# A hybrid decoder step: transposes one projection tile behind, block products ahead of the last ones, six projection banks, and reordered seams in the down projection

## The chip, the cores and the metric

The kernel runs on one core of a Trainium2 chip. The metric is the device time of one execution in microseconds; the median of three runs of the kernel before is 1769.6 us (1768.57 to 1771.12). Lower is better.

## What is computed

The reference is one inference step of a decoder layer for a prompt of 1024 rows and a sample group of 64 rows (8 sequences of 8), model width 1024, in fp32. What matters here is its second part:

```python
x = x + merged @ w_out                                   # output projection
f, conv_state = conv_ffn(rmsnorm(x, norm2_g), ...)       # see below
x = x + f
y = rmsnorm(x, final_norm_g)

def conv_ffn(h, prefix, w_gate, w_up, conv_w, conv_b, w_down):
    g = h @ w_gate                                       # 1024 x 2816
    u = h @ w_up
    gc = conv_b + sum_j conv_w[j] * shifted(g, j)        # causal, width 3
    return (gelu(gc) * u) @ w_down, last two rows of g
```

## The kernel before

**Products.** Each fp32 operand is split into a high part (a cast on ScalarE, L113) and a low part (a subtraction on VectorE, L114). A product runs three passes on TensorE: high by high, high by low, low by high. A weight or activation tile that was split lies in a slot of the tag hl (five slots); what was loaded for it lies in a slot of the tag raw (four slots). Results are summed in PSUM. Until the gate/up loop ends there are two tiles of two banks (tag big), two of one bank (nat), and one each of tp and av, which the transposes use.

**Output projection and second norm (from L950 on).** For each half `nb` of the 1024 output columns the sample (`mm_s`) and the eight prompt tiles (`mm_n`, 24 products each) are projected, each into a nat bank. `add_sq` adds the bank to the residual x (VectorE, L931) and sums its squares on ScalarE (L932), which writes its unused result into the bank. In the second half each tile is then stored to `x1_d` for the end of the kernel, `norm2` normalises it in place (`rstd_of`, seven steps on [128,1] and a square root, then L938), and `put` transposes it, 128 columns at a time, into the stacks B11, B21, B22 and T1 to T4. B are quadrants of the normalised activations; T are sums and differences of them (L989 to L992 on VectorE and GpSimd), since the products use a seven-product scheme on 2 x 2 blocks. T1 and T2 take the slots that the first four tiles' inputs leave, T3 and T4 those of the others. The tiles come in the order 0, 2, 1, 3, 4, 6, 5, 7.

**Gate/up loop.** For 22 rounds `m`, `prep(m)` splits the seven weight pieces a11, s1, s2, a12, s3, s4, a22 (the sums and differences on GpSimd) and `products(m)` runs the block products (`prod`, L1132, 12 TensorE products each) in the order a11 by B11, s1 by T1, s2 by T2, a12 by B21, s3 by T3, s4 by B22, a22 by T4, with ScalarE copies and VectorE adds between them. The products of s1 go to the bank that the code calls c.

**Down projection (`run_steps`).** Seven passes P1, P2, P5, P6, P7, P3, P4, each of 11 steps (k), each step four row tiles of three products (L1298) into four banks of a new pool of seven; P2, P6, P7 and P3 add two products per step for the sample (L1338, bank sb). `prep_down` loads and splits a step four steps ahead. The first four steps of P1 run from raw slots (`k < 4`); the others from the tiles XB and ST, which lie where the loop's pools were. `sum1` and `sum2` form sums and differences for later passes. `evac` takes a pass's banks out: the first at the end of the pass, the others one per step in the next. The banks of P7 are the ones of P6; P3 and P4 take new ones. After P3 the first four row tiles and the sample are normalised (`norm`: ScalarE scales, GpSimd multiplies by the gain and stores). In P4 the last four steps are held back and run row tile by row tile, each followed by its norm on VectorE and its stores.

**What sets the order.** The order on each engine and on the queues of SP and GpSimd is fixed when the kernel is built. A planner takes the source order as priority, and puts an instruction earlier if by its own estimate of times it is ready while those ahead of it are not. On the chip each engine keeps that order.

Of the kernel before, what the change touches and what calls it, by code (L numbers as in the profile page):

```python
# [16 lines left out]
P = 128  # L17
# [15 lines left out]
def hybrid_step(ctx, tc, x_prompt, x_sample, mem_prompt, cache_k, cache_v, page_table, state_pool,  # L33
# [888 lines left out]
    with tc.tile_pool(name="p5", bufs=1, reuse_waits="tile") as p5:  # L922
# [11 lines left out]
        def norm2(xt, n, t):  # L934
# [3 lines left out]
            nc.vector.scalar_tensor_tensor(xt, xt, r, g2b[:n], op0=ALU.mult, op1=ALU.mult)  # L938
# [3 lines left out]
        def put(Bt, xh, a, wide=False):  # L942
# [5 lines left out]
            split(Bt[:, 0, :, a * P:(a + 1) * P], Bt[:, 1, :, a * P:(a + 1) * P], v)  # L948

# [3 lines left out]
        for nb in range(2):  # L953
# [6 lines left out]
            else:  # L960
                nc.sync.dma_start(g2b, bc(norm2_g[0], P))
                raws[0], raws[1] = raw_ffn(0), raw_ffn(1)
            pt = nat()
            mm_s(pt, wf, ms)
            add_sq(x1s, (pt[0:TS], pt[TS:P]), pt[0:TS], TS, NT, nb)
            if nb == 1:
                nc.gpsimd.dma_start(x1s_d, x1s)
                norm2(x1s, TS, NT)
                xs = ap_.tile([P, KT, P], F32R, tag="hs", bufs=1, name="xs")
                to_stack(x1s, xs, KT)  # L970
                nc.gpsimd.tensor_tensor(x1s[:, 0:512], x1s[:, 512:D], x1s[:, 0:512], op=ALU.subtract)
            for i, t in enumerate((0, 2, 1, 3, 4, 6, 5, 7) if nb else range(NT)):
                pt = nat()
                mm_n(pt, wf, macts, t)
                add_sq(x1[t], (pt,), pt, P, t, nb)
                if nb == 0:
                    continue
                nc.gpsimd.dma_start(x1_d[t], x1[t])
                norm2(x1[t], P, t)
                if i == 3:  # L980
                    T1, T2 = [ap_.tile([P, 2, 4, 512], F32R, tag="act", bufs=4, name=f"T{q}") for q in (1, 2)]
                a = t // 2
                if t % 2 == 0:
                    put(B11, x1[t][:, 0:512], a)
                    put(B21, x1[t][:, 512:D], a)
                    continue
                xa, xb = x1[t - 1], x1[t]
                put(B22, xb[:, 512:D], a)
                nc.vector.tensor_tensor(xa[:, 0:512], xb[:, 0:512], xa[:, 0:512], op=ALU.subtract)  # L989
                nc.gpsimd.tensor_tensor(xb[:, 0:512], xb[:, 512:D], xb[:, 0:512], op=ALU.subtract)  # L990
                nc.vector.tensor_tensor(xb[:, 512:D], xb[:, 512:D], xa[:, 0:512], op=ALU.subtract)
                nc.gpsimd.tensor_tensor(xa[:, 512:D], xa[:, 512:D], xb[:, 512:D], op=ALU.subtract)  # L992
                todo.append((xa, xb, a))
                if T1 is not None:
                    for (xa, xb, a) in todo:
                        put(T1, xa[:, 0:512], a)
                        put(T2, xb[:, 512:D], a)
                        late.append((xa, xb, a))
                    todo = []
# [9 lines left out]
    with tc.tile_pool(name="fa", bufs=1, reuse_waits="tile") as fa:  # L1009
# [70 lines left out]
        def prep(m):  # L1080
# [14 lines left out]
            tA = pair("wA")  # L1095
            w["a11"] = piece(tA, 0, a11)
# [10 lines left out]
            w["a12"] = piece(tA, 1, a12)  # L1107
# [21 lines left out]
        def prod(out, wt, Bt, start):  # L1129
            for k in range(4):  # L1130
                for (pw, ph) in PASSES:
                    nc.tensor.matmul(out, wt[:, pw, k], Bt[:, ph, k], start=(start and k == 0 and (pw, ph) == (0, 0)),  # L1132
                                     stop=(k == 3 and (pw, ph) == (1, 0)), skip_group_check=True)

        def products(m, nxt):
            w = wts.pop(m)
            ab = big()
# [12 lines left out]
            prod(a, w["a11"], B11, True)  # L1150
# [8 lines left out]
            prod(b, w["a12"], B21, True)  # L1159
# [70 lines left out]
        def sum1(k):  # L1230
            ld(ST[k][:, 0], fA(1, 1, k))
            if k < 4:
                ld(ST[k][:, 1], wB(0, 0, k))
# [3 lines left out]
        def sum2(k):  # L1237
            if k < 4:
# [9 lines left out]
        def sq(x, junk, i, c):  # L1248
            n = x.shape[0]
            nc.scalar.activation(junk, x, AF.Square, accum_out=ssf[:n, i, c:c + 1])  # L1250

        def norm(x, i, dst, late):
            n = x.shape[0]
            ss = sm.tile([P, 1], F32, tag="ss", name=f"ss{uid()}")[:n]
            tt(ss, ssf[:n, i, 0:1], ssf[:n, i, 1:2], ALU.add)
            r = rstd_of(ss, n, 1.0 / D, 1)
            if late:
                for c in (LO, HI):
                    nc.vector.scalar_tensor_tensor(x[:, c], x[:, c], r, gfb[:n, c], op0=ALU.mult, op1=ALU.mult)
                    nc.sync.dma_start(dst[:, c], x[:, c])  # L1260
            else:
                nc.scalar.activation(x, x, AF.Identity, scale=r)
                nc.gpsimd.tensor_tensor(x, x, gfb[:n], op=ALU.mult)
                nc.gpsimd.dma_start(dst, x)

        def smp2(c, op):
            for h in range(2):
                tt(ys[:, c], ys[:, c], sb[0][h * TS:(h + 1) * TS], op)

        def evac(p, t, b):  # L1270
            y0, y1 = Y[t], Y[t + 4]
            if p == "P1":
                nc.scalar.copy(U[t], b)
            elif p == "P2":
                tt(y0[:, LO], y0[:, LO], b, ALU.add)
                sq(y0[:, LO], b, t, 0)
# [205 lines left out]
```

## Time and profile before

| | |
|---|---|
| median of 3 runs | 1769.6 us |
| profiled execution | 1768.74 us |
| its span, first to last instruction | 1767.0 us |
| mean granted TensorE clock | 0.986 |
| TensorE busy | 1698.4 us, 96% |
| VectorE busy | 952.8 us, 54% |
| ScalarE busy | 723.2 us, 41% |
| GpSimd busy | 412.1 us, 23% |
| chain that ended last, TensorE's share | 84% |

Times in the profile are microseconds from the first instruction. PE is TensorE, DVE is VectorE, ACT is ScalarE, POOL is GpSimd, SP the engine that issues most loads; L12 is line 12 of the kernel. An idle time is put down to what ended it. Products are pipelined, so a run of them is read by its length and count, not by the duration of one.

### The profile page before, as it was taken

The numbers are of one execution on the slowest core, as the hardware profiler recorded it, in microseconds if no ns is written. First come the engines' busy times: TensorE is split into PE (matmuls) and PEld (weight loads), VectorE is DVE, ScalarE is ACT, GpSimd is POOL, SyncE is SP. The second block draws the span as 40 slices with busy tenths as digits, with TensorE's granted clock in tenths as the row PEclk, the third lists the DMA queues.
The fourth block names the chain that finished last, engine by engine and source line by source line (L and its number), as shares of the span: only waits on it lengthen the run. The fifth ranks groups of instructions, "written<-read, shape, count | busy, mean of one in ns | idle before, by whom it ended". The sixth has DMA issues, their size and how long they took to land.

```text
span 1767.0 us, 22904 instructions
## 1 busy us (share of the span) xinstructions
PE 1698.4 (96%) x8157; PEld 1327.8 (75%) x8157; DVE 952.8 (54%) x1648; ACT 723.2 (41%) x1397; POOL 412.1 (23%) x438
## 2 busy tenths in 40 slices
PE   7999999999999999999989899999999999899996
PEld 5887876765666787777768778888888888688875
DVE  6412134330220766676734776666666666578778
ACT  5422234331330766665522354444444444344343
POOL 1113020300200324202200244444444442100003
PEclk9999999999999999999999999999999999999998
DMA  7432251357665424154542132222222222891513
GB/s 272 152 131 82 79 171 59 110 180 237 201 223 193 136 86 142 34 167 155 182 167 66 72 63 72 73 73 73 73 73 72 73 73 84 299 337 49 177 68 137
DMA packets 142359, 228.18 MB, mean 129 GB/s; under 512 B 26703, under 2 KB 64109, under 8 KB 142245
## 3 DMA queue, kind: packets, MB, share of 16 engines
q1 hardware_dynamic: 126453, 178.25, 31.3%
q0 software_dynamic: 15792, 48.48, 8.1%
q8 instruction: 64, 1.05, 0.2%
q14 instruction: 50, 0.41, 0.1%
HBM read 176.19 MB, written 50.54 MB: 128 GB/s over the span
## 4 chain that ended last, share of the span: by engine, by line
PE 84%; DVE 6%; DMA 3%; issue 3%; ACT 2%; SPq 1%; POOL 1%; DVEq 0%; POOLq 0%; ACTq 0%
PE nat L182 18%; PE big L1132 17%; PE P L1298 10%; PE nat L191 8%; PE nat L1132 7%; PE big L182 4%; PE tp L110 4%; PE av L1047 3%; PE big L781 2%; PE av L811 2%; PE nat L199 2%; PE av L110 1%; PE av L571 1%; PE sb L1338 1%; PE big L675 1%
## 5 line engine op out<-in xcount | busy, mean ns | idle before, releaser
L182 PE MATMUL nat<-act,hl 128*128 128x512 f32 x1344 | 359.3, 405 | 0.0
L182 PEld LDWEIGHTS nat<-act,hl 128*128 128x128 f32 x1344 | 242.7, 189 | 62.1 <-issue 15.1
L1298 PE MATMUL P<-hd 128*128 128x512 f32 x924 | 223.7, 397 | 12.9 <-ACT hd L113 6.1
L1298 PEld LDWEIGHTS P<-hd 128*128 128x128 f32 x924 | 176.7, 192 | 52.5 <-ACT hd L113 6.7
L191 PE MATMUL nat<-hl,act 128*128 128x512 f32 x768 | 187.6, 402 | 6.8 <-ACT nat L932 5.1
L191 PEld LDWEIGHTS nat<-hl,act 128*128 128x128 f32 x768 | 146.9, 193 | 39.0 <-ACT nat L932 5.5
L1132 PE MATMUL big<-B,wA 128*128 128x512 f32 x528 | 131.2, 396 | 0.0
L114 DVE TENSOR_TENSOR hl<-raw,hl 128x1024 fp32r<-128x1024 f32 x52 | 66.4, 1288 | 117.1 <-ACT hl L113 115.8
L1132 PEld LDWEIGHTS big<-B,wA 128*128 128x128 f32 x528 | 95.9, 188 | 24.4 <-ACT gu L1157 6.3
L114 DVE TENSOR_TENSOR wB<-stm,wB 128x512 fp32r<-128x512 f32 x44 | 50.7, 1154 | 102.1 <-ACT wB L113 102.1
L474 POOL DMA_DIRECT2D gl<-ev x48 | 26.2, 547 | 280.8 <-ACT ev L473 256.5
L473 ACT COPY ev<-nat 128x512 f32<-128x512 f32 x48 | 28.1, 586 | 116.1 <-PE nat L182 115.6
L1115 POOL TENSOR_TENSOR stm<-rf,stm 128x512 f32<-128x512 f32 x22 | 28.7, 1304 | 188.3 <-DVE wB L114 188.2
L1132 PE MATMUL nat<-B,wC 128*128 128x512 f32 x264 | 70.5, 389 | 0.0
L113 ACT CAST hl<-raw 128x1024 fp32r<-128x1024 f32 x60 | 62.5, 1051 | 16.8 <-PE nat L182 7.9
L1132 PE MATMUL big<-T,wC 128*128 128x512 f32 x264 | 66.4, 400 | 0.0
L114 DVE TENSOR_TENSOR hd<-rd,hd 128x1024 fp32r<-128x1024 f32 x37 | 49.3, 1334 | 30.2 <-ACT hd L113 25.9
L1132 PE MATMUL nat<-T,wB 128*128 128x512 f32 x264 | 64.9, 394 | 0.0
L1132 PE MATMUL big<-T,wD 128*128 128x512 f32 x264 | 64.0, 391 | 0.0
L113 ACT CAST hd<-rd 128x1024 fp32r<-128x1024 f32 x37 | 38.9, 1051 | 60.1 <-PE sb L1338 31.9
L1132 PE MATMUL big<-T,wB 128*128 128x512 f32 x264 | 63.4, 389 | 0.0
L1148 DVE TENSOR_TENSOR gu<-gu,big 128x512 f32<-128x512 f32 x44 | 30.3, 688 | 57.2 <-PE big L1132 57.2
(450 smaller groups left out, 3168.8 us busy)
## 6 DMA issues: line engine op xcount, KB each, us to landing
raw<-in_w_in SPq DMA_DIRECT2D x40, 512.0 KB
kr<-in_cache_k SPq DMA_DIRECT2D x64, 256.0 KB
vr<-in_cache_v SPq DMA_DIRECT2D x64, 256.0 KB
rd<-f_d SPq DMA_DIRECT2D x59, 256.0 KB
gl<-ev POOLq DMA_DIRECT2D x48, 256.0 KB, 2.7
rd<-in_w_ffn_down SPq DMA_DIRECT2D x48, 256.0 KB
rf<-in_w_ffn_gate SPq DMA_DIRECT2D x22, 512.0 KB
rf<-in_w_ffn_up SPq DMA_DIRECT2D x22, 512.0 KB
```

Source lines behind the costliest of these rows:

```text
L110: nc.tensor.transpose(out, in_, ident[:n, :n])
L113: nc.scalar.copy(hi, src)
L114: (lo_eng or nc.vector).tensor_tensor(lo, src, hi.bitcast(F32), op=ALU.subtract)
L182: nc.tensor.matmul(out, wf(k, pw)[:, n0:n0 + P], acts[c][ph][:, k, :], start=(k == ks[0] and (pw, ph) == (0, 0)), stop=(k == ks[-1] and (p ...
L191: nc.tensor.matmul(out, acts[c][ph][:, k, o:o + P], wf(k, pw), start=(k == ks[0] and (pw, ph) == (0, 0)), stop=(k == ks[-1] and (pw, ph) = ...
L199: nc.tensor.matmul(out, stack[:, k, :], wf(k, pw), start=(k == ks[0] and pw == 0), stop=(k == ks[-1] and pw == 1))
L781: nc.tensor.matmul(S[:, k0:k0 + n], Qd[:, m, part, qs], Kst[:, m, k0:k0 + n], start=(part == 0), stop=(part == 1))
L811: nc.tensor.matmul(av[:, :P], aT[:, k * P:(k + 1) * P], vn[:, k0 + k], start=(k0 + k == 0), stop=(k0 + k == i))
L1047: nc.tensor.matmul(pt[:, i * 256:(i + 1) * 256].rearrange("p (h x) -> p h x", h=2), xs[:, k] if k < 4 else st2[:, k - 4], w[n1][:, :, k] i ...
L1132: nc.tensor.matmul(out, wt[:, pw, k], Bt[:, ph, k], start=(start and k == 0 and (pw, ph) == (0, 0)), stop=(k == 3 and (pw, ph) == (1, 0)), ...
L1148: nc.vector.tensor_tensor(hv(g, i), hv(g, i), q(x), op=ALU.add)
L1298: nc.tensor.matmul(banks[t], h[:, ph, 0, t * P:(t + 1) * P], h[:, pw, 1], start=(k == 0 and p not in ("P2", "P7") and (pw, ph) == (0, 0)), ...
```

## The change

In the first half of the output projection, sample and tiles take six banks in turn (two nat, four halves of the two big tiles), and each half of x1 is stored by itself as it is done. In the second half the sum goes to a staging tile `stg` (two of the four raw slots), which the norm reads and which is stored; the loads for the up matrix's first round, so far issued ahead of this half, come with `prep(0)`. The transposes of a tile are written in the source after the next tile's projection, add and norm. Ahead of the last tile's transposes stand the split of a11 and a12 and their two block products of the first round.

In the down projection five steps of P1 (not four) run from raw slots; one step (not four) is written ahead of the sample's leftovers; `evac` hands out single operations, which `more` takes, four at the first step of a pass and one or two at the others; P7's squares no longer go through each bank; the four first norms of P3 are one chain of [128,4] steps, and the scaling is one VectorE instruction with no GpSimd multiply; P4's right halves are multiplied by the gain beforehand, and its norms split the scaling between ScalarE and VectorE.

```diff
-        def add_sq(xt, pts, junk, n, t, nb):
+        def add_sq(xt, pts, junk, n, t, nb, out=None):
             xh = xt[:, nb * 512:(nb + 1) * 512]
+            out = xh if out is None else out
             for q in pts:
-                nc.vector.tensor_tensor(xh, xh, q, op=ALU.add)
-            nc.scalar.activation(junk, xh, AF.Square, accum_out=ssn[:n, t, nb:nb + 1])
+                nc.vector.tensor_tensor(out, xh, q, op=ALU.add)
+            nc.scalar.activation(junk, out, AF.Square, accum_out=ssn[:n, t, nb:nb + 1])
...
+            for (c, src) in ((slice(0, 512), xt[:, 0:512]), (slice(512, D), hi)):
+                nc.vector.scalar_tensor_tensor(xt[:, c], src, r, g2b[:n, c], op0=ALU.mult, op1=ALU.mult)
+        def obank(nb):
+            obc[0] += 1
+            if nb or obc[0] % 6 in (1, 2):
+                return nat()
+            if not obs:
+                pt = big()
+                obs.extend((pt[:, 0], pt[:, 1]))
+            return obs.pop(0)
...
-                raws[0], raws[1] = raw_ffn(0), raw_ffn(1)
-            pt = nat()
+                raws[0] = raw_ffn(0)
+                stg = [wp.tile([P, 2, 512], F32, tag="raw", bufs=4, name=f"stg{i}") for i in range(2)]
+            pt = obank(nb)
...
             for i, t in enumerate((0, 2, 1, 3, 4, 6, 5, 7) if nb else range(NT)):
-                pt = nat()
+                pt = obank(nb)
                 mm_n(pt, wf, macts, t)
-                add_sq(x1[t], (pt,), pt, P, t, nb)
                 if nb == 0:
+                    add_sq(x1[t], (pt,), pt, P, t, nb)
+                    nc.gpsimd.dma_start(x1_d[t][:, 0:512], x1[t][:, 0:512])
                     continue
-                nc.gpsimd.dma_start(x1_d[t], x1[t])
-                norm2(x1[t], P, t)
+                hi = stg[i % 4 // 2][:, i % 2]
+                add_sq(x1[t], (pt,), pt, P, t, nb, hi)
+                nc.gpsimd.dma_start(x1_d[t][:, 512:D], hi)
+                norm2(x1[t], P, t, hi)
+                if i == 6:
+                    tA0 = wp.tile([P, 2, 2, 4, P], F32R, tag="hl", bufs=5, name="wA0")
+                    for q in range(2):
+                        split(tA0[:, q, 0], tA0[:, q, 1], raws[0][q][:, :, 0:P])
+                behind.pop()()
...
+                if i == 7:
+                    ab0 = big()
+                    prod(ab0[:, 0], tA0[:, 0], B11, True)
+                    prod(ab0[:, 1], tA0[:, 1], B21, True)
+                def puts(t=t, a=t // 2):
...
+                behind.append(puts)
+        behind.pop()()
...
-                if k < 4:
+                if k < 5:
                     src = rawt(fA(0, 0, k), wB(0, 0, k))
...
+        def norm(xs_, i, dsts):
+            n, w = xs_[0].shape[0], len(xs_)
+            ss = sm.tile([P, w], F32, tag=f"rs_s{w}", bufs=1, name=f"ss{uid()}")[:n]
+            tt(ss, ssf[:n, 0, i:i + w], ssf[:n, 1, i:i + w], ALU.add)
+            r = rstd_of(ss, n, 1.0 / D, w)
+            for j, (x, dst) in enumerate(zip(xs_, dsts)):
+                def go(x=x, dst=dst, j=j):
+                    nc.vector.scalar_tensor_tensor(x, x, r[:, j:j + 1], gfb[:n], op0=ALU.mult, op1=ALU.mult)
+                    nc.gpsimd.dma_start(dst, x)
+                yield go
+        def last(t, b):
+            y, i = Y[t + 4], t + 4
+            tt(y[:, LO], y[:, LO], b, ALU.add)
+            sq(y[:, LO], b, i, 0)
...
+            nc.scalar.activation(y[:, HI], y[:, HI], AF.Identity, scale=r)
+            nc.sync.dma_start(dst[:, HI], y[:, HI])
+            nc.vector.scalar_tensor_tensor(y[:, LO], y[:, LO], r, gfb[:, LO], op0=ALU.mult, op1=ALU.mult)
+            nc.sync.dma_start(dst[:, LO], y[:, LO])
...
             elif p == "P7":
-                tt(U[t], U[t], b, ALU.add)
-                tt(y1[:, HI], y1[:, HI], U[t], ALU.subtract)
-                sq(y1[:, HI], b, t + 4, 1)
-                tt(y1[:, LO], y1[:, LO], U[t], ALU.add)
+                yield lambda: tt(U[0], U[0], bk[0], A)
+                for h in range(2):
+                    yield lambda h=h: smp1(LO, S, h, sbk)
+                    yield lambda h=h: smp1(HI, A, h, sbk)
+                for t in range(1, 4):
+                    yield lambda t=t: tt(U[t], U[t], bk[t], A)
+                for t in range(4):
+                    yield lambda t=t: tt(Y[t + 4][:, HI], Y[t + 4][:, HI], U[t], S)
+                    yield lambda t=t: (sq(Y[t + 4][:, HI], bk[3], t + 4, 1), tt(Y[t + 4][:, LO], Y[t + 4][:, LO], U[t], A))
+                sq(ys[:, LO], bk[3][0:TS], NT, 0)
             elif p == "P3":
...
+                yield from norm([Y[t] for t in range(4)], 0, [y_prompt[t * P:(t + 1) * P] for t in range(4)])
+                for t in range(4):
+                    yield lambda t=t: tt(Y[t + 4][:, HI], Y[t + 4][:, HI], gfb[:, HI], ALU.mult)
+                nc.vector.tensor_scalar(ssf[:, 1, 4:8], ssf[:, 1, 4:8], 1.0 / D, EPS, op0=ALU.mult, op1=A)
+                yield from norm([ys], NT, [y_sample])
...
-                    if pend:
-                        evac(*pend.pop(0))
+                    more(4 if k == 0 else 1 if p != "P3" and p != "P4" or k > 6 else 2)
...
-        run_steps(0, 4)
+        prep_down(4)
+        run_steps(0, 1)
```

## Rows read from the trace of the kernel before

**Rows 1.** Waits, TensorE: engine, line, releaser; total us, times, longest.

```profile
PE P L1298 <- ACT hd L113: 6.1, 2, 5.6
PE nat L191 <- ACT nat L932: 5.1, 1, 5.1
PE P L1298 <- DVE hd L114: 4.5, 2, 4.3
PE av L110 <- DVE x L938: 2.9, 1, 2.9
PE P L1298 <- ACT P L1250: 2.3, 1, 2.3
```

**Rows 2.** Stretches: length, busy us (instructions) of each engine, granted clock, DMA.

```profile
908.00:912.00 4.00, 3.81 (x9) 3.04 (x10) 0.00 (x0) 0.75 (x4) 0.00 (x0) 0.50 1.03 411
...
949.18:1032.88 83.70, 74.52 (x373) 59.28 (x372) 61.97 (x130) 31.85 (x71) 25.02 (x24) 0.96 0.27 73
...
1030.00:1490.00 460.00, 459.60 (x2164) 372.06 (x2162) 292.56 (x375) 197.71 (x363) 190.27 (x168) 1.00 0.25 75
...
1520.00:1590.00 70.00, 65.03 (x279) 53.51 (x280) 52.76 (x55) 32.55 (x47) 1.07 (x2) 0.95 0.98 348
```

**Rows 3.** TensorE in order of time, projection: start, us, operation, count, idle before.

```profile
908.19 41.16 PE L191 MATMUL nat<-hl,act 128*128 128x512 f32 x168 [5.11 <-ACT nat L932]
...
1008.34 0.71 PE L1132 MATMUL big<-B,wA 128*128 128x512 f32 x2
...
1027.07 1.06 PE L1132 MATMUL nat<-T,wB 128*128 128x512 f32 x2
...
1032.88 2.88 PE L1132 MATMUL big<-T,wB 128*128 128x512 f32 x12
```

**Rows 4.** VectorE in order of time, around the last projection tile.

```profile
1010.01 0.68 DVE L931 TENSOR_TENSOR x<-x,nat 128x512 f32<-128x512 f32 x1
...
1015.02 1.28 DVE L938 SCALAR_TENSOR_TENSOR x<-x,rsy,g2b 128x1024 f32<-128x1024 f32 x1
```

**Rows 5.** TensorE in order of time, down projection.

```profile
1507.06 11.34 PE L1298 MATMUL P<-hd 128*128 128x512 f32 x48
...
1524.97 23.81 PE L1298 MATMUL P<-hd 128*128 128x512 f32 x96 [5.57 <-ACT hd L113]
...
1580.80 32.80 PE L1298 MATMUL P<-hd 128*128 128x512 f32 x144
...
1685.34 6.86 PE L1298 MATMUL P<-hd 128*128 128x512 f32 x22 [2.32 <-ACT P L1250]
...
1719.69 20.11 PE L1298 MATMUL P<-hd 128*128 128x512 f32 x88
...
1746.04 11.64 PE L1298 MATMUL P<-hd 128*128 128x512 f32 x41 [4.34 <-DVE hd L114]
```

**Rows 6.** ScalarE in order of time, casts of XB in the first down pass.

```profile
1523.79 0.61 ACT L113 CAST hd<-XB 128x512 fp32r<-128x512 f32 x1
...
1531.13 0.62 ACT L113 CAST hd<-XB 128x512 fp32r<-128x512 f32 x1 [1.44 <-DMA XB<-f_d]
```

**Rows 7.** VectorE in order of time, from the seam of P7 to the end.

```profile
1682.65 1.28 DVE L1197 TENSOR_TENSOR uy<-uy,P 128x512 f32<-128x512 f32 x2
...
1738.69 1.22 DVE L114 TENSOR_TENSOR hd<-rd,hd 128x1024 fp32r<-128x1024 f32 x1
...
1742.62 4.50 DVE L114 TENSOR_TENSOR hd<-rd,hd 128x1024 fp32r<-128x1024 f32 x2
...
1760.73 0.15 DVE L1197 TENSOR_TENSOR ss<-ssf 128x1 f32<-128x1 f32 x1
```

**Rows 8.** Groups by line, 1712 to 1768: busy us, mean ns; idle before.

```profile
L1263 POOL TENSOR_TENSOR yy<-yy,uy 128x1024 f32<-128x1024 f32 x4 | 11.5, 2894 | 205.5 <-ACT rst L121 205.1 <-ACT yy L1262 0.4
L1259 DVE SCALAR_TENSOR_TENSOR yy<-yy,rsy,uy 128x512 f32<-128x512 f32 x8 | 5.6, 747 | 0.1
```

**Rows 9.** Groups by line, GpSimd, 949 to 1033, the same columns.

```profile
L990 POOL TENSOR_TENSOR x<-x 128x512 f32<-128x512 f32 x4 | 5.1, 1287 | 15.3 <-DVE x L989 15.3
```

More of the change, by code (lines that the diff above doesn't have):

```diff
@@ L948, in put, with prod @@
             split(Bt[:, 0, :, a * P:(a + 1) * P], Bt[:, 1, :, a * P:(a + 1) * P], v)
+        def prod(out, wt, Bt, start):
+            for k in range(4):
+                for (pw, ph) in PASSES:
+                    nc.tensor.matmul(out, wt[:, pw, k], Bt[:, ph, k], start=(start and k == 0 and (pw, ph) == (0, 0)),
+                                     stop=(k == 3 and (pw, ph) == (1, 0)), skip_group_check=True)
         raws = {}
@@ L1094, in prep @@
             w = wts[m] = {}
-            tA = pair("wA")
-            w["a11"] = piece(tA, 0, a11)
+            tA = pair("wA") if m else tA0
+            w["a11"] = piece(tA, 0, a11) if m else tA[:, 0]
             yield
@@ L1106, in prep @@
             yield
-            w["a12"] = piece(tA, 1, a12)
+            w["a12"] = piece(tA, 1, a12) if m else tA[:, 1]
             yield
@@ L1127, in prep @@
             late_s.extend([smp_])
[L1129 to L1133, printed above, removed]
         def products(m, nxt):
             w = wts.pop(m)
-            ab = big()
+            ab = big() if m else ab0
             a, b, c = ab[:, 0], ab[:, 1], nat()
@@ L1158, in products @@
             next(nxt, None)
-            prod(b, w["a12"], B21, True)
+            if m:
+                prod(b, w["a12"], B21, True)
             acc(g0, 0, b)
@@ L1249, in sq @@
             n = x.shape[0]
[L1250 to L1264, printed above, removed]
@@ L1300, in mm4, with more @@
                                  stop=(k == KH - 1 and (pw, ph) == (1, 0)), skip_group_check=True)
+        def more(n):
+            while n and pend:
+                f = next(pend[0], None)
+                if f is None:
+                    pend.pop(0)
+                    continue
+                f()
+                n -= 1
         def run_steps(s0, s1):
-            for g in range(4, s0 + 4 if s0 else 0):
-                prep_down(g)
             for s in range(s0, s1):
@@ L1341, in run_steps @@
                     continue
-                now = 4 if p in ("P1", "P6") else 1
-                for t in range(4):
-                    if t < now:
-                        evac(p, t, banks[t])
-                    else:
-                        pend.append((p, t, banks[t]))
-                if p == "P6":
-                    smp2(LO, ALU.add)
-                if p == "P7":
-                    smp2(LO, ALU.subtract)
-                    smp2(HI, ALU.add)
-                    sq(ys[:, LO], sb[0][0:TS], NT, 0)
-                if p == "P3":
-                    smp2(HI, ALU.add)
-                    sq(ys[:, HI], sb[0][0:TS], NT, 1)
-                    norm(ys, NT, y_sample, False)
+                pend.append(evac(p, list(banks), sb[0]))
+                more(1)
             if s1 == len(steps):
@@ L1361, in run_steps @@
                         mm4("P4", k, t, h)
-                    evac("P4", t, banks[t])
+                    if t == 0:
+                        more(99)
+                    last(t, banks[t])
         S1AT = {4 + (13 * k) // 10: k for k in range(KH)}
```

111 lines of the change are left out of this document (65 added, 46 removed).

## The prediction

> **What bounds the kernel now.** TensorE does. First I read the stretches [rows 2]: in the gate/up loop it is busy 459.60 of 460 us at full clock, with VectorE at 292.56 and GpSimd at 190.27. What comes off ahead of the loop moves the end one for one, and nothing inside it can be had. So I looked where TensorE waits [rows 1]: one wait of 5.1 us on ScalarE at L932 (the output projection), 2.9 us on VectorE at L938 (the second norm), 5.6 us on ScalarE's cast at L113 and 2.3 us at L1250, 4.3 us on VectorE's split at L114 (the down projection). Then its order in time [rows 3, 5] shows a second loss behind each long wait. The pace at full clock is 144 products in 32.80 us [rows 5], 0.227 us each; after the 5.1 us wait 168 products take 41.16 us [rows 3], 3.0 more than 38.1, and the granted clock there is 0.50, the 1.2 GHz level, against 2.4 [rows 2]. After the 2.3 us wait 22 products take 6.86 us instead of 5.0 (1.9 lost), after the one at L113 96 take 23.81 instead of 21.8 (2.0 lost), after the last 41 take 11.64 instead of 9.3 (2.3 lost) [rows 5]. I count wait and slow stretch together.
>
> **The change part by part.** The sum is against the profiled execution, 1768.74 us (span 1767.0).
>
> *Six banks in the first half of the projection.* The second prompt tile has to wait for the sample's bank, which waits for x_sample to land: 5.11 us, then 3.0 at the low clock [rows 3]. Now the sample and tile 0 sit in the two nat banks, tiles 1 to 4 in four halves of two big banks; the first reuse is tile 5, some 5 x 5.45 = 27 us after tile 0 starts, long past the 5.1 us. The big tiles are free: the gate stage's last products are over before. Eight stores of 256 KB are added on GpSimd's queue, idle here, and the second half's become half as large. Gain 8.1; if the clock fell all the same 5.1.
>
> *Transposes one tile behind, two block products ahead of the last ones.* The stretch from the second half's first product to 1032.88, where TensorE becomes continuous, is 83.70 us: TensorE busy 74.52, so 9.2 waiting, VectorE 61.97 [rows 2]. The last projection product ends at about 1008.2. VectorE adds that tile only at 1010.01 (splits of earlier transposes stand ahead of it) and has it normalised at 1015.02 + 1.28 = 1016.3, 8 us later [rows 4]; product c starts at 1027.07, 19 us after the projection [rows 3]. After the change add and norm come ahead of the previous tile's transposes: 0.69 + a square + seven small steps + 1.3, about 5 us. Under them TensorE has 24 block products (5.4 us; 12 of them are there now, as the row at 1008.34 shows) and the transposes of the tile before. What VectorE then has to do until c is the last pair's two differences, its three splits, T3 and T4's eight, the sample's and one weight's: the whole between projection and c sums, with the norm, to some 19 splits, adds and differences at 0.61 (0.69 less the overlap of 0.08 with the next), plus 2.0 for norm and small steps: 13.6, say 14 us with gaps, against 19. So: 5.0 from the chain, 2.7 for the a12 product (12 x 0.227) that then lies in the gap, 1.6 because c (5.8 us from 1027.07 to 1032.88 for 12 products and 16 short ones) runs less at the low clock, and 1.7 of the short waits before 1008 that are part of the 9.2. Sum 11.0. Bounds: 2.7, if the chain still ends when it does now (and 0 if the 24 products, in TensorE's fixed order, hold up a transpose by as much), and 9.2 + 2.7 + 1.6 = 13.5 if every wait goes. I take 11.0, since the row at 1010.01 shows 2 us of pure queueing. Writing the second half of x1 to a staging buffer and storing it from there frees the norm from waiting for that store; no term of its own. The staging takes two of the four raw slots, so the up matrix's first tiles (1 MB) load only behind the last store; the first product with them comes five products of 2.7 after c starts, some 28 us past the projection. I cost that at nothing; if SP's plan set these loads behind the small conv-weight loads, the cover shrinks but is not gone.
>
> One thing speaks against this part. The two scalings that now end the norm (0.75 each [rows 8]) have two SBUF inputs, and beside them GpSimd will be at the differences of the pair before, two of 1.29 us [rows 9]. VectorE's splits, with two SBUF inputs too, took 4.50 us for two beside GpSimd against 1.22 for one [rows 7]. If both scalings are held by a whole difference, the norm is 2.6 us later and this term is 8.4. I take none of it, because the scalings come in the planner's order ahead of those differences. The Trainium skill (SBUF — State Buffer, Who interferes with whom) says that VectorE with two SBUF inputs and GpSimd reading SBUF exclude each other for a whole instruction, whichever comes first; by that the sum is 26.7, by the order that I assume 29.3. The 4.50 us agree with the rule; no row shows this overlap.
>
> *Fifth step of the first down pass from a raw slot, rest of the first steps later.* Before, four steps run (1507.06, 48 products in 11.34), then the sample's transposes and a chain of splits, then ScalarE reaches the casts of XB at 1523.79 and TensorE resumes at 1524.97 [rows 5, 6], idle for 5.6 [rows 1]. The chain moves up by three steps, but the XB loads don't: they are issued when the old pool is free, and arrive at 348 GB/s [rows 2], 1.5 us for a step's two of 256 KB; the seventh step's cast at 1531.13 waited for them [rows 6]. So I take the new fifth step as cover (2.7 us) and the sixth as starting when the fifth does now: gain 2.7, and the low clock stays. Bounds: 0, if pass two, fed by a saturated DMA, is reached early and waits (from 1520 to 1590 the DMA is busy 0.98 of the time [rows 2]), and 7.6 = 5.6 + 2.0 if the loads land early. Two transfers move to before 1507; two more come back in the sums of that step.
>
> *Seams of the down passes.* At P7 to P3 TensorE waits for the fourth bank: add, subtract and square on P7's first bank. Now the bank is free after the first add, and VectorE starts that at 1682.65 [rows 7], ending 1683.3, while TensorE ran dry at 1683.0. That leaves 0.3, and I add 0.6 for the sample's bank (four adds of 0.6 queued right behind). Gain 2.3 + 1.9 - 0.9 = 3.3; bounds 0.5 and 4.2. At P2 to P5 the first square now follows the next split: 0 to 1 us, taken as 0 (L1250 shows one wait in all [rows 1], the one at P7).
>
> *Last pass and tail.* The prompt's first four tiles lose the GpSimd multiply (2.9 us each [rows 8]). While those run VectorE is blocked: two splits took 4.50 us against 1.22 for one [rows 7]. But VectorE gets their scaling: counted from the end of P3 (1719.7) until the last split it has 7 x (0.69 + 1.22), 3 + 2 adds of 0.69, 5 scalings of 1.28, 4 gain multiplies of 0.69 and two small chains of 1.1: 28.2 us, or 24.8 with each overlapping its successor by 0.08 and the chains filled; today the last split ends at 1742.62 + 4.50 = 1747.1, 27.4 after. I take 25.6, 1.8 less. TensorE still waits, and its low clock stays. In the tail the last tile's sums start at 1760.73, 3.05 us after the last product (1757.68) [rows 5, 7]; add and square need 1.5 of them, the rest queues behind the third tile's two scalings. Now there is one on VectorE and one on ScalarE: 1.5 + 0.75 + a small add = 2.4. Gain 1.8 + 2.4 = 4.2; bounds -2 (split sum 28.2 and clock as now) and 9.7 (5.0 wait, 2.3 clock, 2.4).
>
> Sum: 8.1 + 11.0 + 2.7 + 3.3 + 4.2 = 29.3. 1768.74 - 29.3 = 1739.4; the median of the runs, 1769.6, is 0.9 above the profiled execution, so 1740.3, called 1740.
>
> **Rivals.** *The last tile's chain still ends last.* The order on each engine is a planner's, and the row at 1008.34 shows that it already pulls block products ahead of transposes, so the new order in the source may be partly there. Then only 2.7 + 1.7 of the 11.0 come: 1769.6 - 22.7 = 1747. Against it: the add that is 2 us late. That is also the case in which the change doesn't do what it says.
>
> *The down half gives nothing.* DMA holds the second pass, and the norms that moved to VectorE hold the last: 2.7, 3.3 and 4.2 go, 1769.6 - 19.1 = 1750.5. For it: the two VectorE sums, 24.8 and 28.2, lie on both sides of 27.4. Against it: the tail's 2.4 and L1250 have their own rows.
>
> *More goes than I took*: the loads of the sixth step land early (4.9 more) and the last pass loses its wait (4.1 more): 1731.
>
> *Slower.* Slots of raw, hl and big tiles are handed on in turn, and the change shifts who has them when the loop begins. If the planner's order then had TensorE wait once in each of the 22 block rounds, a wait of over 1.33 us would take back 29.3; at 1.6 us it is 35 us, 1775. From 1.5 us a round on the kernel is slower than before by more than 0.2%. Nothing in [rows 2] speaks for it: 0.4 us in 460, VectorE a third free.
>
> *GpSimd's differences hold the norm* (above): 29.3 - 2.6, 1742.9. For it the 4.50 us, against it the order.
>
> **How the numbers follow.** Forecast 0.49; chain 0.21; down half 0.12; GpSimd 0.05; more 0.07; slower 0.04; mishaps that cancel all 0.02. The likeliest is 1740. The sum's ends are 5.1 + 0 + 0 + 0.5 - 2 = 3.6 and 8.1 + 13.5 + 7.6 + 4.2 + 9.7 = 43.1, so 1766 and 1726.5; all terms at one end together is less than 2 in 10, and I take 1728 to 1756, which holds every case but the slower one and the mishaps. Within 0.2% (3.5 us, about what this measurement can tell from no change) 0.03, slower 0.04, faster 0.93.
>
> **What would show it.** Right: no wait at L932's line and clock 1.00 near 910; c within 15 us of the last projection product; one step more before the wait ahead of XB; at most 1 us between P7 and P3; no GpSimd arithmetic in the last pass and its last split 25 to 26 us after P3; the last tile's sums about 1.5 us behind the last product, not 3.05. Wrong: block products ahead of transposes that then come as late as now; waits on rd loads in the second down pass; a wait in each block round; a split in the last pass later than 27 us.

## The result and the profile after

The changed kernel takes 1745.74 us (median of 4, 1742.85 to 1746.60) where the one before takes 1770.36 beside it: a ratio of 0.9852 (95% interval 0.9837 to 0.9866), 24.6 us less where 29.3 were forecast. In a second set of runs the ratio was 0.9851 (0.9831 to 0.9871). The time lies in the forecast range, but the sum is right for the wrong terms. The profiled execution is 1745.99 us, its span 1744.2.

TensorE's order in time gives the gain by stretches. All are counted from the first product of the projection (897.44 us before, 898.89 after): code that is the same in all put it anywhere from 896.3 to 900.4 in the profiles of this study.

| stretch on TensorE | before | after | gain | forecast |
|---|---|---|---|---|
| first half of the projection | 51.74 | 44.22 | 7.5 | 8.1 |
| second half, to its last product | 58.96 | 56.44 | 2.5 | |
| from there to c | 18.93 | 17.51 | 1.4 | |
| c to the first product of round 1 | 22.41 | 21.64 | 0.8 | 11.0 for these three |
| the loop from there | 457.58 | 457.70 | -0.1 | 0 |
| P1 to P2's first sample product | 41.56 | 39.82 | 1.7 | 2.7 |
| from there to P4 | 171.07 | 169.46 | 1.6 | 3.3 |
| P4's products | 37.99 | 30.61 | 7.4 | 1.8 |
| last product to the end | 9.32 | 7.91 | 1.4 | 2.4 |

They add to 24.2; less the later start of 1.45 that is the 22.8 between the spans.

TensorE in order of time, the changed kernel (start, us, operation, count, idle before):

```profile
898.89 5.61 PE L191 MATMUL nat<-hl,act 128*128 128x512 f32 x24
904.35 16.92 PE L191 MATMUL big<-hl,act 128*128 128x512 f32 x72
...
943.11 3.79 PE L199 MATMUL nat<-hl,ms 128*128 128x512 f32 x16
...
1017.06 0.39 PE L969 MATMUL nat<-T,wB 128*128 128x512 f32 x1
...
1029.36 3.02 PE L969 MATMUL big<-T,wC 128*128 128x512 f32 x12 [1.64 <-DVE gu L1185]
...
1038.70 1.55 PE L969 MATMUL big<-B,wA 128*128 128x512 f32 x6
...
1501.64 0.27 PE L110 MATMUL sb<-ident,gc 128*44 128x128 f32 x1 [1.19 <-DVE fsv L1104]
...
1515.46 20.92 PE L1368 MATMUL P<-hd 128*128 128x512 f32 x84 [3.33 <-ACT hd L113]
...
1705.68 21.70 PE L1368 MATMUL P<-hd 128*128 128x512 f32 x95
1727.57 8.72 PE L1368 MATMUL P<-hd 128*128 128x512 f32 x37 [0.20 <-DVE hd L114]
```

The 5.11 us wait of [rows 3] is gone, and so is the 4.34 us wait in P4 [rows 5]; 5.57 became 3.33 and 1.19. Stretches of the same kernel (length, busy time of each engine, granted clock, DMA share, GB/s):

```profile
904.00:912.00 8.00, 7.86 (x35) 6.20 (x34) 2.75 (x4) 2.06 (x6) 1.10 (x2) 1.00 1.02 336
...
1017.06:1023.25 6.19, 5.82 (x22) 4.19 (x21) 6.19 (x6) 3.62 (x7) 4.85 (x4) 0.72 0.91 8
...
1515.46:1525.00 9.54, 9.54 (x35) 7.75 (x36) 8.86 (x13) 6.07 (x10) 0.00 (x0) 0.82 1.04 377
...
1727.50:1736.30 8.80, 8.72 (x37) 6.87 (x37) 5.61 (x21) 3.79 (x11) 0.00 (x0) 1.00 0.30 94
```

Near 910 the clock is 1.00 where [rows 2] have 0.50, and full at the end too; in c (0.72) and at the sixth step (0.82) part still runs at the 1.2 GHz level.

VectorE between the projection and round 1, and at the end:

```profile
999.60 0.69 DVE L932 TENSOR_TENSOR stg<-x,nat 128x512 f32<-128x512 f32 x1 [0.60 <-PE nat L191]
...
1001.60 0.89 DVE L937 TENSOR_TENSOR ss<-ssn 128x1 f32<-128x1 f32 x1
...
1005.29 0.75 DVE L943 SCALAR_TENSOR_TENSOR x<-stg,rsy,g2b 128x512 f32<-128x512 f32 x1
1005.95 0.68 DVE L1029 TENSOR_TENSOR x<-x,x 128x512 f32<-128x512 f32 x1
1008.09 0.69 DVE L1031 TENSOR_TENSOR x<-x,x 128x512 f32<-128x512 f32 x1 [1.45 <-POOL x L1030]
...
1010.81 0.69 DVE L114 TENSOR_TENSOR T<-av,T 128x512 fp32r<-128x512 f32 x1 [0.24 <-ACT T L113]
...
1015.87 0.41 DVE L114 TENSOR_TENSOR xd<-tp,xd 128x256 fp32r<-128x256 f32 x1
...
1017.98 1.77 DVE L114 TENSOR_TENSOR wC<-stm,wC 128x512 fp32r<-128x512 f32 x1
...
1028.63 0.67 DVE L1185 TENSOR_TENSOR gu<-gu,big 128x512 f32<-128x512 f32 x1
...
1689.44 0.68 DVE L1236 TENSOR_TENSOR yy<-yy,uy 128x512 f32<-128x512 f32 x1
...
1726.31 1.21 DVE L114 TENSOR_TENSOR hd<-rd,hd 128x1024 fp32r<-128x1024 f32 x1
...
1738.09 0.21 DVE L1310 TENSOR_SCALAR rsa<-ssf 128x1 f32<-128x1 f32 x1
```

The last norm ends at 1006.0, 6.5 us after the projection (8 before). Then VectorE stands 1.45 us for a difference on GpSimd, and has twelve splits until c (the last at 1015.87). The last gain multiply (1689.44; the gain lies in the tile uy) falls into P3; the last split of P4 ends at 1727.5, 21.8 us behind P3's end (27.4 before, 25.6 forecast). TensorE waited 0.20 us for it.

### The profile page after: what moved, and what is told of

Same layout as the page of the kernel before. It is cut to its first block, busy times and chain, and to the rows that moved or that the text cites. A ratio compares the mean times of both kernels' runs of the same rounds, so it can differ in the third digit from the quotient of the medians.

```text
span 1744.2 us, 22910 instructions
## 1 busy us (share of the span) xinstructions
PE 1691.7 (97%) x8157; PEld 1323.2 (76%) x8157; DVE 950.4 (54%) x1636; ACT 719.0 (41%) x1392; POOL 402.0 (23%) x441
## 4 chain that ended last, share of the span: by engine, by line
PE 83%; DVE 6%; DMA 4%; issue 3%; ACT 2%; POOL 1%; SPq 1%; ACTq 0%; POOLq 0%; DVEq 0%
PE nat L182 18%; PE big L969 17%; PE P L1368 9%; PE nat L191 7%; PE nat L969 7%; PE big L182 4%; PE tp L110 4%; PE av L1090 3%; PE big L781 2%; PE av L811 2%; PE nat L199 2%; PE av L110 1%; PE big L191 1%; PE sb L1414 1%; PE av L571 1%
## 5 line engine op out<-in xcount | busy, mean ns | idle before, releaser
L191 PE MATMUL nat<-hl,act 128*128 128x512 f32 x648 | 155.5, 396 | 1.8 <-DVE act L114 1.0
L191 PEld LDWEIGHTS nat<-hl,act 128*128 128x128 f32 x648 | 121.7, 190 | 28.0 <-DVE act L114 1.8
L969 PEld LDWEIGHTS big<-T,wC 128*128 128x128 f32 x264 | 47.8, 188 | 17.5 <-DVE gu L1185 8.3
```

Source lines behind the costliest of these rows:

```text
L191: nc.tensor.matmul(out, acts[c][ph][:, k, o:o + P], wf(k, pw), start=(k == ks[0] and (pw, ph) == (0, 0)), stop=(k == ks[-1] and (pw, ph) = ...
```

## Experiments

Theory: the six banks gave their term; behind the projection VectorE still decides, so c and round 0 come hardly sooner; the last pass gained because GpSimd's multiplies are gone. The rivals stand in the expectation of each run. Ratios are to the kernel before; what the runs can't tell apart is read from stretches, which repeat: the changed kernel's 139.81 us from the first projection product to round 1 was 140.00 in its second profile and 139.58 to 140.65 in five other kernels that leave this stretch as it is.

### The parts by themselves

```diff
-            pt = nat()
+            pt = obank(nb)
             mm_s(pt, wf, ms)
...
-                pt = nat()
+                pt = obank(nb)
                 mm_n(pt, wf, macts, t)
```

> The kernel before with the six banks of the first half of the projection alone. If the lead that the changed kernel has when the second half begins (7.5 us counted from the first half's start) stays to the end: 1770.4 - 7.5 = 1763, and no wait after the first tile. Rival: what comes off here is given back in the second half, where VectorE's queue of splits ends last whenever TensorE comes: less than 4 us, 1767 or more.

Ratio 0.9936 (0.9919 to 0.9953), 1763.16 us beside 1773.52. Round 1 comes 144.42 us after the first projection product, 7.6 sooner than before's 152.04. The first theory holds: the term of the banks reaches the loop undiminished. The runs give 8.3 to 14.3 us; what they have beyond the stretch was not followed up. The profile has less, a span 4.3 us shorter than before's: with the same code there, TensorE waits 3.42 us at P7's end, not 2.32, and the 22 products behind take 8.14 us, not 6.86.

The changed kernel above the line `KH = NF // 2`, the kernel before from there on:

```diff
-        prep_down(4)
-        run_steps(0, 1)
+        run_steps(0, 4)
...
-                pend.append(evac(p, list(banks), sb[0]))
-                more(1)
+                now = 4 if p in ("P1", "P6") else 1
...
```

> The changed kernel with the down projection of the kernel before, so the banks, the transposes one tile behind and the two early block products. If the leads read from the trace are right (10.7 us when the loop ends, 12.1 with the 1.45 us that the changed kernel's profiled execution was late before the projection): 1770.4 - 12.1 = 1758. Rival: the early part is worth what was forecast (8.1 + 11.0) and the trace gives it too little: 1770.4 - 19.1 = 1751.

Ratio 0.9918 (0.9901 to 0.9936), 14.5 us (11.3 to 17.5); to the start of P1 it is 11.4 us faster than before (598.21 against 609.62). Both exclude the 19.1 of the forecast: the upper half is worth about 11 us by the stretch, 14.5 by the runs.

```diff
-                if i == 6:
-                    tA0 = wp.tile([P, 2, 2, 4, P], F32R, tag="hl", bufs=5, name="wA0")
...
-                if i == 7:
-                    ab0 = big()
-                    prod(ab0[:, 0], tA0[:, 0], B11, True)
-                    prod(ab0[:, 1], tA0[:, 1], B21, True)
```

> The changed kernel without the split and the two block products ahead of the last transposes (they come in the loop as before); the transposes stay one tile behind. If VectorE's queue sets when the first product of s1 starts, TensorE has idle time there and the 24 products are free: their removal costs the 12 of a12 and the 12 of a11, 2.7 to 5.4 us, less the 1.6 us wait at the first round that they brought: 1745.7 + 1.1 to 3.8, 1747 to 1749.5. Rival: 18 of them stand in TensorE's order ahead of the last transposes until 1006.40, and hold these up: no difference or faster, 1742 to 1746.

Ratio 0.9848 (0.9831 to 0.9864): the runs show no difference to the changed kernel. The stretch does: 143.31 us to round 1 instead of 139.8. So the two early products are worth 3.5 us, and of the transposes one tile behind, without them, 144.42 - 143.31 = 1.1 us is left.

### The sixth step of the first down pass

```diff
+                    if s == 8:
+                        nc.vector.tensor_copy(ylo[0][:, :, 0:1], XB[8][:, 0, 0:4].rearrange("p (a x) -> p a x", x=1))
+                        nc.vector.tensor_copy(uy[:, 2048:4096:1024], XB[8][:, 0, 0:2])
                     if 8 <= s < 12:
```

> The changed kernel with six loads of 1.75 MB (the residual's first halves, the sample's, the last gain) made to wait until the down projection's step 8 has its tile, by two small copies into them, so that the loads of XB for the sixth step stand ahead of them on SP's queue. If this queue order is what left TensorE waiting 3.33 us at the sixth step and at the low clock behind it: XB comes about 5 us sooner, the wait and the 1.9 us of the low clock go: 1745.7 - 5 = 1740.7. Rival: the loads are bound by the DMA engines in any order, or TensorE waits later for what was put off: within 1 us, 1745 to 1747.

Ratio 0.9804 (0.9787 to 0.9821), 1739.83 us, faster than the changed kernel. P1 to P2's first sample product takes 34.57 us; with the changed kernel's order it was 39.6 to 41.7 in eight profiles, with the old one 41.5 to 41.7 in three. SP's queue, ScalarE and TensorE of this kernel:

```profile
1503.15 0.78 SPq L1226 DMA_DIRECT2D XB<-f_d  x1
```

```profile
1508.53 0.62 ACT L113 CAST hd<-XB 128x512 fp32r<-128x512 f32 x1 [1.58 <-DMA XB<-f_d]
```

```profile
1502.22 29.50 PE L1368 MATMUL P<-hd 128*128 128x512 f32 x129
```

The same issue and cast in the changed kernel, with the loads ahead of them:

```profile
1501.32 0.33 SPq L1226 DMA_DIRECT2D rd<-f_d  x1
...
1502.56 2.48 SPq L1226 DMA_DIRECT2D yy<-x_d  x4
1505.13 1.45 SPq L1226 DMA_DIRECT2D uy<-x1s_d  x1
1506.63 0.58 SPq L1226 DMA_DIRECT2D uy<-in_final_norm_g  x1
1507.37 0.32 SPq L1226 DMA_DIRECT2D XB<-f_d  x1
```

```profile
1514.19 0.62 ACT L113 CAST hd<-XB 128x512 fp32r<-128x512 f32 x1 [7.80 <-DMA XB<-f_d]
```

Counted from P1's start the cast comes 6.2 us sooner (11.5, 17.8), and 129 products run without a wait. The cause of the wait was not the DMA's rate but six loads (1502.56 to 1507.21) that nobody needed yet, ahead on the queue: 4.8 of the 6.2 us are the issue of XB itself (10.97 and 6.16 us from P1's start), the rest passes between issue and cast. The Trainium skill (DMA: Bandwidth & Descriptors, Two DMAs through the same engine are not ordered) says that within a queue of one DMA engine descriptors start in order though they need not finish so; these rows show the order of issue on SP, and no run here shows that of the descriptors.

```diff
-        run_steps(0, 1)
+        run_steps(0, 2)
...
+        prep_down(5)
-        run_steps(1, len(steps))
+        run_steps(2, len(steps))
```

> The kernel with the XB loads first, with two steps of the first down pass (not one) ahead of the sample's leftovers. TensorE waits 1.2 us there for VectorE's multiply into fsv, which stands behind two splits of 3.1 us each (beside GpSimd's last multiplies). If 2.7 us more of cover is enough: 1.2 us less from the pass's first product to the next pass's, 1738.6 where the other had 1739.8. Rival: the sample's chain of splits then ends 2.7 us later and TensorE waits at the sixth step: no change or up to 2 us slower.

On top of the loads: the stretch falls to 33.25 us, 1.3 less, as the first theory has it. The ratio, 0.9809 (0.9793 to 0.9825), can't tell it from 0.9804.

### What holds c and round 0

```diff
+                    s0 = stg[0][:, 0].rearrange("p (k x) -> p k x", k=4)
+                    nc.gpsimd.tensor_tensor(s0, raws[0][0][:, :, P:256], raws[0][1][:, :, P:256], op=ALU.add)
+                    split(tB0[:, 0, 0], tB0[:, 0, 1], s0)
...
+        c0 = nat()
+        prod(c0, tB0[:, 0], T1, True)
         for (xa, xb, a) in late:
-            put(T3, xb[:, 0:512], a, True)
-            put(T4, xa[:, 512:D], a, True)
+            put(T3, xb[:, 0:512], a)
+            put(T4, xa[:, 512:D], a)
```

> The changed kernel with the first product of s1 (bank c) ahead of the last pair's T3 and T4: the s1 weight of round 0 is summed and split while the last tile is projected, T3 and T4 of the first three pairs come ahead of the last tile's transposes. Nothing is added or left out but one sum on GpSimd. If the order of VectorE's queue is what holds c (12 splits stand between the last norm at 1006.0 and c at 1017.06): c starts after three of them, and of the 5 us that TensorE waits between 999.5 and 1038.7, and the 1.6 of low clock, 3 to 5 go: 1741 where the changed kernel has 1745. Rival: the amount of VectorE's work holds it, in whatever order (15.8 us busy of the 17.6 from the end of the projection to c): within 1 us of the changed kernel.

Ratio 0.9847 (0.9830 to 0.9863): nothing. c starts 4.3 us sooner, 113.9 us after the first projection product instead of 118.2, yet round 1 comes at 140.26. The same edits with c behind those transposes:

```diff
-        c0 = nat()
-        prod(c0, tB0[:, 0], T1, True)
         for (xa, xb, a) in late:
...
+        c0 = nat()
+        prod(c0, tB0[:, 0], T1, True)
```

> As the experiment with c ahead of the last pair's T3 and T4, but with c behind these transposes again in the source; the s1 weight stays split early, and T3 and T4 of the first three pairs stay ahead of the last tile's transposes. There c came 4.3 us earlier and round 1 did not, for VectorE stood idle for 5.8 us behind transposes that c had pushed back. If the order on TensorE is what cost it: c comes some 3 us earlier than in the changed kernel and round 1 starts 1.5 to 3 us earlier, 137 to 138.3 us after the first projection product, 1743. Rival: splits and GpSimd's sums hold round 0 in any order: 139.3 to 140.3, 1745 to 1746.

Ratio 0.9860 (0.9844 to 0.9877); c at 114.5, round 1 at 140.10. The rival's number holds, and the forecast had followed the wrong chain: an earlier c is lost again before round 1. TensorE and VectorE of this kernel:

```profile
1015.45 2.79 PE L969 MATMUL nat<-T,wB 128*128 128x512 f32 x11
1018.17 0.46 PE L110 MATMUL tp<-ident,x1s 64*128 64x64 f32 x4
```

```profile
1019.08 0.42 DVE L114 TENSOR_TENSOR xd<-tp,xd 128x256 fp32r<-128x256 f32 x1 [2.03 <-ACT xd L113]
...
1020.57 0.69 DVE L114 TENSOR_TENSOR wB<-stm,wB 128x512 fp32r<-128x512 f32 x1 [1.07 <-ACT wB L113]
```

Here too c's products ran ahead of a transpose, the sample's, and VectorE stood 2.03 and 1.07 us for what came behind it. So the order on TensorE isn't excluded as a part of the cause; the two runs show only that c 4 us earlier brought nothing in either order. What GpSimd's sums cost round 0 is told by leaving four of them out:

```diff
-            s1 = stm()
-            nc.gpsimd.tensor_tensor(s1, a21, a22, op=ALU.add)
+            if m == 1:
+                s1 = a21
+            else:
+                s1 = stm()
+                nc.gpsimd.tensor_tensor(s1, a21, a22, op=ALU.add)
...
```

> The changed kernel without GpSimd's four sums of weights for round 1 of the gate/up loop (the pieces are split straight from the loaded tile, so round 1 computes with wrong weights; all else is as it was). In the changed kernel VectorE's splits of weights between 1018 and 1027 take 1.77 us each beside these sums, not 0.69, and TensorE waits 0.30 and 1.64 us in round 0 and runs part of it at the low clock. If that contention is what gives back the early a12 product: from the first projection product to the first product of round 1 it is 2 to 2.5 us less than the 139.8 of the changed kernel, and the time about 1743.5. Rival: the chain ahead of c sets round 0 too: within 0.5 us of 139.8.

Ratio 0.9836 (0.9818 to 0.9853), which the runs can't tell from the changed kernel. Round 1 comes at 136.75, 3.1 us sooner, more than expected. VectorE and TensorE of this kernel:

```profile
1018.58 0.68 DVE L114 TENSOR_TENSOR wD<-rf,wD 128x512 fp32r<-128x512 f32 x1
1019.18 0.68 DVE L114 TENSOR_TENSOR wC<-stm,wC 128x512 fp32r<-128x512 f32 x1
```

```profile
1025.36 2.98 PE L969 MATMUL big<-T,wC 128*128 128x512 f32 x12
...
1034.66 2.91 PE L969 MATMUL big<-B,wA 128*128 128x512 f32 x12
```

Four weight splits of 1.77 to 1.79 us now take 0.67 or 0.68 each, and the 1.64 us wait is gone. In the changed kernel VectorE was never idle between 1016.77 and 1031.60, so it was the length of these splits that counted, not a wait for the sums' results. The kernel before already had such splits, where the forecast could have read them:

```profile
1027.64 1.77 DVE L114 TENSOR_TENSOR wC<-stm,wC 128x512 fp32r<-128x512 f32 x1
```

The Trainium skill (SBUF — State Buffer, Who interferes with whom) says that VectorE with two SBUF inputs and GpSimd reading SBUF exclude each other, while VectorE with one SBUF input doesn't contend; the rows agree on both: the weight splits are held, the split at 1010.81, which reads PSUM, took 0.69 beside a GpSimd sum.

### The last pass

```diff
+                one = sm.tile([P, 1], F32, tag="one", bufs=1, name="one")
+                nc.vector.tensor_scalar(one, Y[3][:, 0:1], 0.0, 1.0, op0=ALU.mult, op1=A)
                 for t in range(4):
-                    yield lambda t=t: tt(Y[t + 4][:, HI], Y[t + 4][:, HI], gfb[:, HI], ALU.mult)
+                    yield lambda t=t: nc.vector.scalar_tensor_tensor(Y[t + 4][:, HI], Y[t + 4][:, HI], one, gfb[:, HI], op0=ALU.mult, op1=ALU.mult)
```

> The changed kernel with the four gain multiplies of P4's right halves made to wait for the norms of P3 (a factor of one, formed from a normalised tile), so that they fall into the last pass, where the forecast had put them. If their running early, in P3, is why the last split came 21.8 us behind P3 and not 25.6: 4 x 0.67 = 2.7 us come back there, TensorE waits 2.9 instead of 0.2, and has up to 2.3 us of low clock behind it: 2.7 to 5 us over the changed kernel, 1748 to 1751. Rival: the last pass gained because GpSimd no longer stops VectorE, and VectorE has room for the four: less than 1 us.

Ratio 0.9860 (0.9842 to 0.9878), 1749.23 us beside 1745.69 for the changed kernel on the same chip. The two intervals overlap. The first theory is right about VectorE alone: the last split does come 24.6 us behind P3, 2.8 later, yet P4's products take 30.63 us as without it. TensorE and VectorE of this kernel:

```profile
1709.34 22.60 PE L1370 MATMUL P<-hd 128*128 128x512 f32 x99
1732.16 7.81 PE L1370 MATMUL P<-hd 128*128 128x512 f32 x33 [0.21 <-ACT hd L113]
```

```profile
1732.75 1.21 DVE L114 TENSOR_TENSOR hd<-rd,hd 128x1024 fp32r<-128x1024 f32 x1
```

TensorE goes on 1.8 us before this split ends; in the changed kernel it waited until its last split ended. So the planner had put other products of P4 ahead of those that need the split. In this order TensorE can stand a last split at 24.6 us; whether the changed kernel's own order needed the multiplies' early place, no run shows. What set the medians 3.5 us apart lies outside this pass and was not settled; in the profile the projection already starts 3.2 us later than in the changed kernel's of that set (900.4, 897.2).

```diff
-                    nc.vector.scalar_tensor_tensor(x, x, r[:, j:j + 1], gfb[:n], op0=ALU.mult, op1=ALU.mult)
+                    nc.scalar.activation(x, x, AF.Identity, scale=r[:, j:j + 1])
+                    nc.gpsimd.tensor_tensor(x, x, gfb[:n], op=ALU.mult)
                     nc.gpsimd.dma_start(dst, x)
```

> The changed kernel with the five norms after P3 scaled as before, by ScalarE and a GpSimd multiply (2.8 to 3.1 us each, 14 us), in the changed order. VectorE has 5 x 1.2 = 6 us less to do. If VectorE stands still beside these multiplies, as two splits of 4.50 us beside one of them say: the last split comes 25 to 28 us behind P3 again, TensorE waits 3 to 6 and goes to the low clock: 4 to 8 us over the changed kernel, 1749 to 1753. Rival: VectorE's own load counts: no difference, or up to 1 us faster.

Ratio 0.9880 (0.9860 to 0.9900), 6.5 us over the changed kernel. P4's products take 38.03 us again, all of the 7.4. VectorE, GpSimd and TensorE of this kernel:

```profile
1717.49 6.30 DVE L114 TENSOR_TENSOR hd<-rd,hd 128x1024 fp32r<-128x1024 f32 x1
```

```profile
1717.93 4.77 POOL L1299 TENSOR_TENSOR yy<-yy,uy 128x1024 f32<-128x1024 f32 x2
```

```profile
1727.91 0.98 PE L1369 MATMUL P<-hd 128*128 128x512 f32 x3 [3.10 <-DVE hd L114]
...
1731.01 11.04 PE L1369 MATMUL P<-hd 128*128 128x512 f32 x38 [0.31 <-DVE hd L114]
```

One split takes 6.30 us instead of 1.22 while two multiplies run.

### A version with all of it

```diff
+            if after is not None:
+                nc.vector.tensor_copy(r[:, 0, 0:1], after)
...
+            if m == 0:
+                raws[1] = raw_ffn(1, tB[:, 1, 1, 0, 0:1].bitcast(F32))
...
-                more(1)
+                more(5 if p == "P7" else 1)
```

> The kernel with the XB loads first and two steps ahead of the sample's leftovers, and two more edits. The up matrix's loads for round 1 wait for the second split of round 0's wB (a copy of one column into the tiles), so that GpSimd's sums of round 1 start behind the splits of round 0 and not beside them; and the sample's four adds of P7 stand ahead of the next split. If VectorE beside GpSimd's sums is what round 0 waits for: 2 to 3 us fewer from the first projection product to round 1 (137 to 138 instead of 139.8); if the sample's bank waits for the split between its adds: the 1.3 us wait at the sample's bank in P7 to P3 goes. Together 3 to 4 us under the 1737.6 of the kernel without them, 1734. Rival: round 1's splits are then late and TensorE waits for them in round 1, and the sample's adds hold up U's: no gain, 1737 to 1739.

Ratio 0.9865 (0.9849 to 0.9881), 1747.13 us: some 10 us worse than without the two edits, beyond the rival too. Round 1 comes at 146.59.

```profile
1029.46 0.69 DVE L114 TENSOR_TENSOR wA<-rf,wA 128x512 fp32r<-128x512 f32 x1 [5.72 <-ACT wA L113]
1030.07 0.68 DVE L1189 TENSOR_TENSOR gu<-gu,big 128x512 f32<-128x512 f32 x1
```

```profile
1030.81 4.56 PE L971 MATMUL big<-T,wC 128*128 128x512 f32 x12 [3.39 <-DVE gu L1189]
```

The delayed loads land too late, VectorE stands 5.72 us for round 1's first weight, and round 0's add of bank b stands behind it. The copies were done at 1020.28, but SP issued these loads from 1023.48 on, behind two small ones. The splits of round 0 did run at 0.68.

```profile
1669.82 1.28 DVE L1240 TENSOR_TENSOR uy<-uy,P 128x512 f32<-128x512 f32 x2
1671.02 2.60 DVE L1240 TENSOR_TENSOR uy<-uy,sb 64x512 f32<-64x512 f32 x4
```

At P7's end the sample's bank still waits 1.20 us, behind a split, two adds of U and its own four; from P2's first sample product to P4 it is 0.9 shorter (168.75 against 169.61). The best kernels are those with the XB loads first, 1739.83 and 1737.61 us.

## Why the prediction was right, and where it was wrong

*Six banks*: right, 7.5 of 8.1.

*Transposes and early products*: 4.7 of 11.0. In its number this is the first rival (2.7 + 1.7), not the forecast. The step "say 14 us with gaps, against 19" failed: it was 17.5. The count of some 19 splits, adds and differences agrees with the trace: VectorE has 19 from 999.60 to the sample's split at 1015.87. Four of them, 2.4 us, are the tile before's last difference and three splits, which the change itself pushes behind the projection and which the forecast's list doesn't name. Too small were the gaps, 2.0 us, 1.45 of them for GpSimd's difference; the norm with its small steps, 3.2 us for 2.0; and the time from the end of the sample's split to c, 0.8, which was not counted. The step behind it failed worse: c was taken for the end of the chain. Made 4 us earlier in two experiments, it brought round 1 no sooner. In the changed kernel round 0's splits beside GpSimd's sums hold it, 3.1 us by the run without four sums; in the two experiments VectorE also stood for transposes behind c, and the two shares were not separated. The 1.6 us of low clock stayed (c ran at 0.72 over 6.19 us, before at 0.73 over 5.81), and of the 2.7 for a12 1.64 came back as a wait. The split of the terms was wrong too: the transposes alone bring 1.1, the early products 3.5. The rival that GpSimd's differences hold the norm: the scalings ran at 0.75 unhindered, as assumed, and only a small sum took 0.89 instead of 0.15. What that rule held up was elsewhere, in round 0, where the forecast had not looked for it.

*Fifth step*: 1.7 of 2.7 in this profile, 0 to 1.9 over eight. The step "the sixth as starting when the fifth does now" failed: counted from P1's start that was 17.9 us, and the sixth step started at 19.1. That the XB loads don't move was wrong. Before, the first was issued 6.23 us after P1's start, now 10.97:

```profile
1513.29 0.54 SPq L1187 DMA_DIRECT2D XB<-f_d  x1
```

The six loads stood ahead of it before, too. Now the fifth step's own raw loads (1501.32) stand ahead of these, and the forecast had not looked at the queue's order.

*P7 to P3*: 1.6 of 3.3; 0.69 and 1.29 us of wait remain instead of 0.3 and 0.6. VectorE started the first add 0.05 us before TensorE ran dry, where the forecast had 0.35; that is the first excess. For the second, the count had the sample's four adds right behind one add of U. In the changed kernel a second add of U and a split stand among them; in the last experiment, with the split gone from there, the sample's bank waited 1.20 all the same, and the second add's 0.6 is the excess over the forecast.

*Last pass*: 7.4 of 1.8. The sum of VectorE's work, 25.6, was 3.8 too long: 2.8 of it are the gain multiplies, which the planner ran in P3 (with them in the last pass the split came at 24.6, near the forecast's lower sum of 24.8). With the last split 5.6 us sooner and not 1.8, "TensorE still waits" failed, and the wait and the low clock both went. That the multiplies taken off GpSimd are the cause is shown, since all of the 7.4 is lost when they are put back there; how much hangs on the gain multiplies' early place is open, as TensorE's order changed with it. *Tail*: 1.4 of 2.4, since the last sums start 1.8 us behind the last product and the end follows 7.9 behind it.

So 6 too many in the upper half and 6 too few in the last pass cancelled, by luck, and the other four terms, 0.6 to 1.7 short each, are the rest of the difference to 29.3.

## What to carry to other kernels

Before an edit is credited with an earlier start, follow the chain past it to the point where the bound engine becomes continuous, and list what that edit pushes behind the point. Price a VectorE instruction with two SBUF inputs by what GpSimd does at that time, and look there first for a wait. Where a queue is in order, look at what stands ahead of the late load before blaming bandwidth.

## What was not expected of the hardware

A stretch of identical code between the same two products repeated within 0.15 us over 457 us (457.56 to 457.70 in 14 profiles), while the time before the projection varied by 4 us. After the wait at the sixth step the granted clock came back sooner in one profile than in the next of the same kernel: 0.82 over 9.54 us after 3.33 us of wait, 0.72 over 10.49 us after 4.00; the 84 products took 20.92 and 22.11 us. That is 1.2 of the 1.8 us between the two (39.82 and 41.65), and the longer wait is the rest. Why the wait itself differs was left open. The stretch of the second profile:

```profile
1514.51:1525.00 10.49, 10.49 (x34) 8.43 (x35) 9.67 (x13) 6.88 (x11) 0.00 (x0) 0.72 1.05 377
```
